# A two-layer decoder trunk in split fp32 on one core: one-function Gelu, an earlier spatial turn, earlier sums, and one more Strassen unit in the last pair

## The chip, the cores and the metric

The kernel runs on one core of a Trainium2 chip. The time is the device time of that core in microseconds (us), the median over several executions. TensorE (PE) does the matrix products, VectorE (DVE) and ScalarE (ACT) prepare their operands and take up their results, GpSimd (POOL) and SyncE (SP) mainly issue DMAs. "L245" is line 245 of the kernel before; an executed instruction carries the line that recorded it.

## The reference

Tokens x (256 x 2048, fp32) go through two layers:

```python
def chunked_sgu(uv, w_s, b_s, ln_g, ln_b):
    ...
    u, v = uv[..., :SGU_WIDTH], uv[..., SGU_WIDTH:]
    ... # vn: v normalised in each group of 128 channels, times ln_g, plus ln_b
    w = jnp.where(tri[None], w_s, jnp.zeros_like(w_s))
    s = jnp.einsum('gij,bnjgd->bnigd', w, vc) + jnp.transpose(b_s)[None, None, :, :, None]
    return u * s.reshape(B, S, SGU_WIDTH)

for l in range(DEPTH):
    h = rms_norm(x, mix_norm[l])
    q, k, v, uv, gate_logits = jnp.split(h @ w_in[l], cuts, axis=-1)
    ... # q and k: norm and rotation
    branch_a = sliding_window_attention(q, k, v, sinks[l]) @ w_attn_branch[l]
    branch_b = chunked_sgu(jax.nn.gelu(uv), w_spatial[l], b_spatial[l],
                           sgu_ln_g[l], sgu_ln_b[l]) @ w_sgu_branch[l]
    gates = jax.nn.sigmoid(gate_logits)
    merged = gates[..., :D_MODEL] * branch_a + gates[..., D_MODEL:] * branch_b
    x = x + merged @ w_out[l]
    h2 = rms_norm(x, ffn_norm[l])
    x = x + (jax.nn.silu(h2 @ w_gate[l]) * (h2 @ w_up[l])) @ w_down[l]
```

`jax.nn.gelu` is here the form with a tanh: 0.5 x (1 + tanh(0.798 (x + 0.0447 x^3))).

## The kernel before, in words

**Products.** All large products run in fp32 accuracy by a high and a low part of each operand. A weight half of 256 rows by 512 columns is one *entry*: its DMA (L218, 512 KB, on SP) fills `raw`, ScalarE rounds it to `whi` (L244), VectorE subtracts to get `wlo` (L245), and TensorE multiplies the stationary activation parts `uh` and `ul` with them (add_product, L340 and L341): six matmuls of 128x512 for one tile of 128 tokens (hi*hi, hi*lo and lo*hi for two blocks of 128 rows), so 12 for both tiles. The pool of `whi` and `wlo` has four buffers (W_SPLIT = 4): the split of an entry starts when TensorE has finished the entry four places earlier.

**Strassen units.** A *unit* is 512 rows of weights against a pair of column chunks, done by seven products of six matmuls (P1 to P7, 42) in place of eight (48). Its weight sums are made by VectorE (L229), its activation sums by `transposed` (L421 to L509): `flat` (L480), `whole` (uh on ScalarE and ul on VectorE, L484 and L485), four `sums` on VectorE (L499), and `finished` (sh on ScalarE, sl on VectorE, L484 and L485). After P5 ScalarE copies the accumulators (L363 to `kept`, L364 to the other accumulator), after P6 and P7 VectorE adds to `kept` (L366). A block that is in no unit has only `uh` and `ul`, made in two halves (ScalarE L435, VectorE L436). `pair` builds the entries of two column chunks; with `two=True` it takes two units.

**Time slots.** `tick()` closes a slot of 12 matmuls, `after(n, fn)` records `fn` n slots later. `wino=` gives six such delays, for the two halves of `flat`, `whole`, the two pairs of `sums`, and `finished`. TensorE's instructions run in the order in which they are recorded; on the other engines a scheduler sets the order when the program is built, and each engine then keeps to it.

**A layer.** First the input projection, with attention and the gating unit worked in between. Class `Spatial` has the gating unit: for the two chunks of v and of u it copies half of the scaled projection from PSUM (L811) and forms Gelu with a Square (L818) and a Tanh (L821) on ScalarE and two operations on VectorE (L819, L822), for each of the two token tiles apart. v is normalised (`center`, `scaled`, `shifted`, L835 to L856), and `mix` multiplies with the transposed spatial weights. These come from `spatial` (L648 to L654): eight transposes by TensorE into `pw` and two VectorE copies to `wsT`. Attention turns its probabilities on TensorE as well (`ppt`, L783); `pw` and `ppt` share two PSUM buffers. Then the branch products, the output projection, and the feed-forward part in three rounds of 4, 4 and 3 chunks of 512 (ROUNDS): `hidden` makes each chunk of the hidden activations (silu L981, product L985/L986), turns it, and after each round `residual` multiplies with `w_down` in two pairs of column chunks and adds to the residual `xs` (L888). In the last round there are three blocks, of which the first (WINO = 0) is a Strassen unit.

Of the kernel before, what the change touches and what calls it, by code (L numbers as in the profile page):

```python
# [10 lines left out]
AF = mybir.ActivationFunctionType  # L11
# [4 lines left out]
NT = 2  # L16
# [21 lines left out]
WINO_MIX = 6, 7, 9, 10, 11, 13  # L38
WINO_HID = 7, 8, 17, 18, 19, 20
W_SPLIT = 4  # L40
W_TWO = 24
# [11 lines left out]
              for early in ([(("q", 1),), (("gate", 0),)], [(("q", 1), ("gate", 0))])]  # L53
GELU_A = 0.044715
GELU_C = 0.7978845608028654


@with_exitstack
def hybrid_trunk(ctx: ExitStack, tc: tile.TileContext, x, mix_norm, w_in, q_norm, k_norm, sinks,
# [101 lines left out]
    for l in range(DEPTH):  # L161
# [14 lines left out]
        for r, (f0, f1) in enumerate(ROUNDS):  # L176
            for f in range(f0, f1):
                plans.append(pair(("ffn", l), w_gate[l, :, f * CW:(f + 1) * CW], w_up[l, :, f * CW:(f + 1) * CW], f == 0,
                                  two=r > 0 and f - f0 < 3))
            c_ = cols_of(w_down[l, f0 * CW:f1 * CW, :], NCH)  # L180
            plans += [pair(("hid", l, r), c_[j], c_[j + 1], j == 0) for j in range(0, NCH, 2)]
    entries = []
# [79 lines left out]
    def after(n, fn):  # L262
        steps.append((slot_no[0] + n, fn))
# [399 lines left out]
    def fetch_large(pl):  # L663
        for n, i in ((13, 2), (17, 3), (21, 0), (25, 1)):
            after(n, lambda i=i: pl.fetch(i))
        after(40, pl.spatial)

# [132 lines left out]
    class Spatial:  # L800
# [5 lines left out]

        def half(self, ps, name):

            dst = slot([P, NT, CW], name=name)
            for t in range(NT):  # L810
                nc.scalar.activation(dst[:, t, :], ps[t], AF.Copy, scale=self.nrm.rh[t])  # L811
            return dst

        def gelu(self, dst, t):

            xh = dst[:, t, :]
            sq = temp(name="sq")
            nc.scalar.activation(sq, xh, AF.Square, scale=2.0)  # L818
            nc.vector.scalar_tensor_tensor(out=sq, in0=sq, scalar=1.0 / GELU_A, in1=xh,  # L819
                                           op0=ALU.add, op1=ALU.mult)  # L820
            nc.scalar.activation(sq, sq, AF.Tanh, scale=2.0 * GELU_C * GELU_A)  # L821
            nc.vector.scalar_tensor_tensor(out=xh, in0=sq, scalar=1.0, in1=xh, op0=ALU.add, op1=ALU.mult)  # L822

        def v(self, c, ps):
            self.vt[c] = vt = self.half(ps, "v")
            for t in range(NT):
                after(1 + t, lambda t=t: self.gelu(vt, t))
                after(4 + 3 * t, lambda t=t: self.center(c, t))
# [29 lines left out]
        def u(self, c, ps):  # L858
            ut = self.half(ps, "u")
            for t in range(NT):  # L860
                after(1 + t, lambda t=t: self.gelu(ut, t))
            for b in range(2):
                after(12 + 3 * b, lambda b=b: self.mix(c, b, ut))
            after(18 + 6 * c, lambda: transposed(self.sguT, c, ut, queue=nc.sync))
# [45 lines left out]
    for l in range(DEPTH):  # L910
# [65 lines left out]
        def hidden(hT, c):  # L976
# [6 lines left out]
            def on_up(up):  # L983
                for t in range(NT):
                    nc.vector.scalar_tensor_tensor(out=hid[:, t, :], in0=up[t], scalar=norm.r[t], in1=hid[:, t, :],  # L985
                                                   op0=ALU.mult, op1=ALU.mult)  # L986
                pe, soon = c == len(hT) - 1 == 2, c == 3
                after(3 if pe else 1 if soon else 2,
                      lambda: transposed(hT, c, hid, on_pe=pe, wino=WINO_HID if c == WINO else None,
                                         queue=None if soon else nc.gpsimd, late=-2 if soon else 0))  # L990
# [52 lines left out]
```

## Time and profile before

| | |
|---|---|
| Time, median of 3 executions | 2457.51 us (2455.78 to 2459.42) |
| The profiled execution's own time | 2457.45 us |
| Its span, first to last instruction | 2455.7 us |
| TensorE busy | 2438.1 us, 99% |
| VectorE busy | 1999.5 us, 81% |
| ScalarE busy | 1472.5 us, 60% |
| DMA | 506.74 MB, 206 GB/s on average |

Rows of the profile name the line, the engine, the operation, output and inputs (buffer numbers left out), the count and the mean of one; what stands in brackets or behind the last bar is the idle time of that engine before the instruction and what it waited for. A matmul's own duration (about 0.39 us) overlaps the next; the distance of their starts is what one costs. The columns of the windows view are busy time and count for each engine, then the granted clock of TensorE, the DMA share and GB/s.

### The profile page before, as it was taken

The numbers are of one execution on the slowest core, as the hardware profiler recorded it, in microseconds if no ns is written. First come the engines' busy times: TensorE is split into PE (matmuls) and PEld (weight loads), VectorE is DVE, ScalarE is ACT, GpSimd is POOL, SyncE is SP. The second block draws the span as 40 slices with busy tenths as digits, with TensorE's granted clock in tenths as the row PEclk, the third lists the DMA queues.
The fourth block names the chain that finished last, engine by engine and source line by source line (L and its number), as shares of the span: only waits on it lengthen the run. The fifth ranks groups of instructions, "written<-read, shape, count | busy, mean of one in ns | idle before, by whom it ended". The sixth has DMA issues, their size and how long they took to land.

```text
span 2455.7 us, 31363 instructions
## 1 busy us (share of the span) xinstructions
PE 2438.1 (99%) x10968; PEld 2012.6 (82%) x10968; DVE 1999.5 (81%) x2320; ACT 1472.5 (60%) x1842; POOL 315.6 (13%) x592
## 2 busy tenths in 40 slices
PE   9999999999999999999999999999999999999999
PEld 7888888888888888887887888888888888888877
DVE  6798676797978997899877986768878789978996
ACT  5567544576655665566655665545666556655664
POOL 3100002132210111001101000021322101110110
PEclk9999999999999999999999999999999999999999
DMA  9555657576667657665747446675767675667654
GB/s 299 196 187 163 212 198 220 186 236 210 220 217 233 210 176 231 230 203 170 229 155 257 152 157 223 202 215 177 246 202 236 204 245 189 200 209 241 203 179 139
DMA packets 280782, 506.74 MB, mean 206 GB/s; under 512 B 28272, under 2 KB 40144, under 8 KB 280624
## 3 DMA queue, kind: packets, MB, share of 16 engines
q1 hardware_dynamic: 262544, 486.35, 61.0%
q0 software_dynamic: 17760, 18.12, 2.8%
q8 instruction: 86, 1.41, 0.2%
q14 instruction: 72, 0.59, 0.1%
q10 hardware_dynamic: 320, 0.27, 0.0%
HBM read 475.27 MB, written 2.10 MB: 194 GB/s over the span
## 4 chain that ended last, share of the span: by engine, by line
PE 90%; DVE 3%; DMA 3%; SPq 1%; issue 1%; ACT 1%; DVEq 0%; ACTq 0%
PE acc L340 59%; PE acc L341 29%; DMA raw<-in_w_in_dram 2%; DVE wlo L245 2%; SPq L416 1%; ACT whi L244 1%; PE po L793 1%; PE psc L754 0%; PE ppt L783 0%; DVE raw L229 0%; PE psg L871 0%; PE pt L453 0%; DMA raw<-in_w_up_dram 0%; DMA raw<-in_w_down_dram 0%; DVE box L410 0%
## 5 line engine op out<-in xcount | busy, mean ns | idle before, releaser
L244 ACT ACTIVATE whi<-raw 128x1024 fp32r<-128x1024 f32 (+1 forms) x1074 | 1132.0, 1059 | 883.0 <-PE acc L341 623.4
L245 DVE TENSOR_TENSOR wlo<-raw,whi 128x1024 fp32r<-128x1024 f32 (+1 forms) x1075 | 1301.3, 1219 | 399.0 <-ACT whi L244 386.7
L340 PE MATMUL acc<-whi,uh 128*128 128x512 f32 x2994 | 1170.3, 391 | 1.2 <-ACT uh L439 1.2
L340 PE MATMUL acc<-wlo,uh 128*128 128x512 f32 x2994 | 1167.1, 390 | 3.0 <-DVE wlo L245 2.9
L341 PE MATMUL acc<-whi,ul 128*128 128x512 f32 x2994 | 1166.4, 390 | 0.0
L340 PEld LDWEIGHTS acc<-wlo,uh 128*128 128x128 f32 x2994 | 562.6, 188 | 123.2 <-DVE wlo L245 6.0
L340 PEld LDWEIGHTS acc<-whi,uh 128*128 128x128 f32 x2994 | 562.6, 188 | 117.7 <-ACT uh L439 1.4
L341 PEld LDWEIGHTS acc<-whi,ul 128*128 128x128 f32 x2994 | 562.3, 188 | 117.8 <-DVE ul L444 0.5
L416 POOL DMA_DIRECT2D tt<-box x544 | 266.5, 497 | 1697.0 <-ACT whi L244 695.5
L229 DVE TENSOR_TENSOR raw<-raw,raw 128x1024 f32<-128x1024 f32 x236 | 287.8, 1219 | 1.6 <-DMA raw<-in_w_up_dram 0.8
L341 PE MATMUL acc<-whi,sl 128*128 128x512 f32 x472 | 184.0, 390 | 3.2 <-DVE sl L485 3.2
L340 PE MATMUL acc<-whi,sh 128*128 128x512 f32 x472 | 184.8, 392 | 1.7 <-ACT acc L364 1.7
L340 PE MATMUL acc<-wlo,sh 128*128 128x512 f32 x472 | 184.2, 390 | 0.0
L341 PEld LDWEIGHTS acc<-whi,sl 128*128 128x128 f32 x472 | 88.6, 188 | 22.5 <-DVE sl L485 4.0
L340 PEld LDWEIGHTS acc<-whi,sh 128*128 128x128 f32 x472 | 88.6, 188 | 20.9 <-ACT acc L364 2.1
L340 PEld LDWEIGHTS acc<-wlo,sh 128*128 128x128 f32 x472 | 88.7, 188 | 18.0
L366 DVE TENSOR_TENSOR kept<-acc,kept 128x512 f32<-128x512 f32 x94 | 64.3, 684 | 10.1 <-PE acc L341 10.1
L369 ACT ACTIVATE acc<-kept 128x512 f32<-128x512 f32 x94 | 54.9, 586 | 4.3 <-DVE kept L366 4.2
L888 DVE SCALAR_TENSOR_TENSOR xs<-acc,xs 128x512 f32<-128x512 f32 (+1 forms) x66 | 42.0, 668 | 8.4 <-PE acc L341 8.1
L436 DVE TENSOR_TENSOR ul<-tt,uh 128x512 fp32r<-128x512 f32 x52 | 34.0, 684 | 2.9 <-ACT uh L435 2.9
L435 ACT ACTIVATE uh<-tt 128x512 fp32r<-128x512 f32 x52 | 29.8, 618 | 9.4 <-DMA tt<-box 9.4
L312 POOL TENSOR_TENSOR rv<-ve,neg_half 128x4 f32<-128x4 f32 x8 | 11.9, 1486 | 172.9 <-DVE ve L839 159.5
(137 smaller groups left out, 874.8 us busy)
## 6 DMA issues: line engine op xcount, KB each, us to landing
raw<-in_w_in_dram SPq DMA_DIRECT2D x239, 512.0 KB, 4.7
raw<-in_w_gate_dram SPq DMA_DIRECT2D x176, 512.0 KB, 4.4
raw<-in_w_up_dram SPq DMA_DIRECT2D x176, 512.0 KB, 4.9
raw<-in_w_down_dram SPq DMA_DIRECT2D x176, 512.0 KB, 5.0
raw<-in_w_out_dram SPq DMA_DIRECT2D x64, 512.0 KB, 5.0
tt<-box POOLq DMA_DIRECT2D x544, 32.0 KB, 4.2
raw<-in_w_attn_branch_dram SPq DMA_DIRECT2D x32, 512.0 KB, 5.6
raw<-in_w_sgu_branch_dram SPq DMA_DIRECT2D x32, 512.0 KB, 4.4
```

The lines of the kernel that those rows point to most:

```text
L229: self.last = nc.vector.tensor_tensor(out=self.raws[d], in0=self.raws[x], in1=self.raws[y], op=ALU.subtract)
L244: self.high = nc.scalar.activation(hi[:, i, :], raw[:, i, :], AF.Copy)
L245: self.last = nc.vector.tensor_tensor(out=lo[:, i, :], in0=raw[:, i, :], in1=hi[:, i, :].bitcast(F32), op=ALU.subtract)
L340: nc.tensor.matmul(ps, a, part[:, kk, :], start=first and kk + n == 0, stop=False, skip_group_check=True)
L341: nc.tensor.matmul(ps, b, hi[:, kk, :], start=False, stop=kk == 1, skip_group_check=True)
L366: nc.vector.tensor_tensor(out=p.kept[:, int(tag == "P7"), :], in0=a[1], in1=p.kept[:, 1, :], op=ALU.add)
L369: nc.scalar.activation(ps, p.kept[:, t, :], AF.Copy)
L416: q.dma_start(dst[j * B:(j + 1) * B, i], box[i * B:(i + 1) * B, j])
L435: nc.scalar.activation(h, s_, AF.Copy)
L436: nc.vector.tensor_tensor(out=l, in0=s_, in1=h.bitcast(F32), op=ALU.subtract)
L793: nc.tensor.matmul(po[:, h, :], pT[kb][:, h, :], self.kv[:, kb, KVW + g * HD:KVW + (g + 1) * HD], start=kb == 0, stop=kb == t)
L888: nc.vector.scalar_tensor_tensor(out=xs[:, t, sl], in0=sums[t][:, i * w:(i + 1) * w], scalar=scale, in1=xs[:, t, sl], op0=ALU.mult, op1=AL ...
```

## The change

1. `Spatial.half` and the old `gelu` go. The new `gelu` is one activation for each token tile, straight from PSUM with the norm as scale, tile 1 first.
2. `fetch_large` records `pl.spatial` 34 slots on in place of 40.
3. The one unit of a last round (three blocks) gets WINO_END in place of WINO_HID, in both layers.
4. The second pair of column chunks of the last round of the last layer has two units; its second unit is block 1, which takes WINO_END too and so gets `flat`, `whole`, `sums` and `finished` in place of the two halves.

```diff
 WINO_HID = 7, 8, 17, 18, 19, 20
+WINO_END = 7, 8, 12, 13, 14, 15
...
-            plans += [pair(("hid", l, r), c_[j], c_[j + 1], j == 0) for j in range(0, NCH, 2)]
+            plans += [pair(("hid", l, r), c_[j], c_[j + 1], j == 0, two=j > 0 and f1 == NF and l == DEPTH - 1)
+                      for j in range(0, NCH, 2)]
...
-        after(40, pl.spatial)
+        after(34, pl.spatial)
...
-        def half(self, ps, name):
+        def gelu(self, ps, name):
             dst = slot([P, NT, CW], name=name)
+            last = nc.scalar.activation(dst[:, 1, :], ps[1], AF.Gelu_apprx_tanh, scale=self.nrm.r[1])
+            with tc.issue_after(last.ins):
+                nc.scalar.activation(dst[:, 0, :], ps[0], AF.Gelu_apprx_tanh, scale=self.nrm.r[0])
+            return dst
+
+        def v(self, c, ps):
+            self.vt[c] = self.gelu(ps, "v")
             for t in range(NT):
-                nc.scalar.activation(dst[:, t, :], ps[t], AF.Copy, scale=self.nrm.rh[t])
-            return dst
-
-        def gelu(self, dst, t):
-            xh = dst[:, t, :]
-            sq = temp(name="sq")
-            nc.scalar.activation(sq, xh, AF.Square, scale=2.0)
-            nc.vector.scalar_tensor_tensor(out=sq, in0=sq, scalar=1.0 / GELU_A, in1=xh,
-                                           op0=ALU.add, op1=ALU.mult)
-            nc.scalar.activation(sq, sq, AF.Tanh, scale=2.0 * GELU_C * GELU_A)
-            nc.vector.scalar_tensor_tensor(out=xh, in0=sq, scalar=1.0, in1=xh, op0=ALU.add, op1=ALU.mult)
-
-        def v(self, c, ps):
-            self.vt[c] = vt = self.half(ps, "v")
-            for t in range(NT):
-                after(1 + t, lambda t=t: self.gelu(vt, t))
                 after(4 + 3 * t, lambda t=t: self.center(c, t))
...
-            ut = self.half(ps, "u")
-            for t in range(NT):
-                after(1 + t, lambda t=t: self.gelu(ut, t))
+            ut = self.gelu(ps, "u")
...
+                wino = None
+                if c == WINO:
+                    wino = WINO_HID if len(hT) == 4 else WINO_END
+                elif c == WINO + 1 and len(hT) == 3 and l == DEPTH - 1:
+                    wino = WINO_END
                 after(3 if pe else 1 if soon else 2,
-                      lambda: transposed(hT, c, hid, on_pe=pe, wino=WINO_HID if c == WINO else None,
+                      lambda: transposed(hT, c, hid, on_pe=pe, wino=wino,
                                          queue=None if soon else nc.gpsimd, late=-2 if soon else 0))
```

**ScalarE at the first v chunk of layer 2.** Numbers behind names are buffers, and each kernel numbers its own; `whi` are weight splits, `v` the chunk, `pT` and `pr` attention's probabilities, `sq` the scratch of the old Gelu. Before:

```order
L811 ACTIVATE v_11565<-acc_11382,rhalf_2070_10713 128x512
L811 ACTIVATE v_11565<-acc_11383,rhalf_2073_10720 128x512
L244 ACTIVATE whi_11619<-raw_11510 128x1024
L785 ACTIVATE pT_11610<-ppt_11605 128x512
L818 ACTIVATE sq_11612<-v_11565 128x512
L818 ACTIVATE sq_11638<-v_11565 128x512
L244 ACTIVATE whi_11649<-raw_11531 128x1024
L821 ACTIVATE sq_11612<-sq_11612 128x512
L821 ACTIVATE sq_11638<-sq_11638 128x512
L244 ACTIVATE whi_11665<-raw_11510 128x1024
L771 ACTIVATE pr_11581,den_11597<-pr_11581,negm_11592 128x128 x4
L768 ACTIVATE es_11594<-es_11594 128x4
```

After, with an ACT_TABLE_LOAD ahead of the Gelu and another ahead of the next exponentials (L771):

```order
L244 ACTIVATE whi_11522<-raw_11464 128x1024
L810 ACT_TABLE_LOAD
L810 ACTIVATE v_11538<-acc_11343,rstd_2064_10678 128x512
L812 ACTIVATE v_11538<-acc_11342,rstd_2061_10671 128x512
L244 ACTIVATE whi_11574<-raw_11483 128x1024
L785 ACTIVATE pT_11570<-ppt_11565 128x512
L771 ACT_TABLE_LOAD
L771 ACTIVATE pr_11541,den_11557<-pr_11541,negm_11552 128x128 x4
L768 ACTIVATE es_11554<-es_11554 128x4
L244 ACTIVATE whi_11599<-raw_11504 128x1024
L244 ACTIVATE whi_11615<-raw_11483 128x1024
```

Square and Tanh are gone, and the exponentials of the next attention step (L771) now stand ahead of the two next splits rather than behind them. In the whole program ScalarE has 18 table loads in place of 4: one ahead of each of the eight groups of Gelu, and one ahead of the next other function; SP's and GpSimd's lists keep their order except for the last output rows.

**VectorE at the spatial weights of layer 2.** `wsT` is the copy of the turned weights, `q` and `box` belong to the turn of the queries, `psc` are scores. Before:

```order
L245 TENSOR_TENSOR wlo_11494<-raw_11413,whi_11493 128x1024
L245 TENSOR_TENSOR wlo_11515<-raw_11431,whi_11514 128x1024
L245 TENSOR_TENSOR wlo_11534<-raw_11473,whi_11533 128x1024
L245 TENSOR_TENSOR wlo_11550<-raw_11491,whi_11549 128x1024
L654 COPY wsT_11568<-pw_11569 128x512
L654 COPY wsT_11568<-pw_11575 128x512
L758 TENSOR_TENSOR pr_11581<-psc_11582,mask 128x2x128
L245 TENSOR_TENSOR wlo_11620<-raw_11510,whi_11619 128x1024
L758 TENSOR_TENSOR pr_11581<-psc_11586,mask 128x2x128
```

After:

```order
L245 TENSOR_TENSOR wlo_11315<-raw_11254,whi_11314 128x1024
L410 STREAM_TRANSPOSE box_11334<-q_11186 128x4x4x32
L245 TENSOR_TENSOR wlo_11339<-raw_11273,whi_11338 128x1024
L410 STREAM_TRANSPOSE box_11334<-q_11186 128x4x4x32
L245 TENSOR_TENSOR wlo_11376<-raw_11293,whi_11375 128x1024
L654 COPY wsT_11391<-pw_11392 128x512
L654 COPY wsT_11391<-pw_11398 128x512
L245 TENSOR_TENSOR wlo_11407<-raw_11312,whi_11406 128x1024
L758 TENSOR_TENSOR pr_11422<-psc_11423,mask 128x2x128
L758 TENSOR_TENSOR pr_11422<-psc_11427,mask 128x2x128
```

The two copies have moved from behind the scores' step that TensorE's next `ppt` follows to a place some six slots earlier, between two splits; on TensorE the eight transposes into `pw` moved with them, from directly ahead of psc and ppt to between the entries of whi_11295 and whi_11314. In layer 1 TensorE's eight transposes moved in the same way, by six entries.

**VectorE at the end.** The last round of layer 2: `sums`, `sl` and `ul` are the activation sums and low parts of a unit, `hid` the product of L985 (now L973). Before, where the unit's `sl` stood (it serves the entry of whi_20206, its P5):

```order
L499 TENSOR_TENSOR sums_20185<-sums_20185,flat_19932 128x256
L245 TENSOR_TENSOR wlo_20207<-raw_20095,whi_20206 128x1024
L245 TENSOR_TENSOR wlo_20217<-raw_20166,whi_20216 128x1024
L499 TENSOR_TENSOR sums_20185<-flat_19932,sums_20185 128x256
L245 TENSOR_TENSOR wlo_20236<-raw_20188,whi_20235 128x1024
L229 TENSOR_TENSOR raw_20095<-raw_20192,raw_20095 128x1024
L485 TENSOR_TENSOR sl_20230<-sums_20185,sh_20229 128x1024
L245 TENSOR_TENSOR wlo_20256<-raw_20095,whi_20255 128x1024
L245 TENSOR_TENSOR wlo_20271<-raw_20190,whi_20270 128x1024
```

After, the `sl` of block 0 (sl_20018) stands ahead of wlo_20121 and wlo_20131, the splits of the entry before P5 and of P5 itself. Further on the work of the new unit has come in (block 1: ul_20022, sums_20346 and sl_20411):

```order
L366 TENSOR_TENSOR kept_20183<-acc_20146,kept_20183 128x512
L245 TENSOR_TENSOR wlo_20277<-raw_20226,whi_20276 128x1024
L973 TENSOR_SCALAR hid_20006<-acc_20091,rstd_2962_15234,hid_20006 128x512
L245 TENSOR_TENSOR wlo_20288<-raw_20240,whi_20287 128x1024
L973 TENSOR_SCALAR hid_20006<-acc_20092,rstd_2965_15241,hid_20006 128x512
L485 TENSOR_TENSOR ul_20022<-flat_20205,uh_20021 128x1024
L245 TENSOR_TENSOR wlo_20312<-raw_20254,whi_20311 128x1024
...
L499 TENSOR_TENSOR sums_20346<-flat_20205,sums_20346 128x256
L245 TENSOR_TENSOR wlo_20395<-raw_20254,whi_20394 128x1024
L245 TENSOR_TENSOR wlo_20415<-raw_20349,whi_20414 128x1024
L229 TENSOR_TENSOR raw_20240<-raw_20309,raw_20240 128x1024
L485 TENSOR_TENSOR sl_20411<-sums_20346,sh_20410 128x1024
```

Between the two pieces stand five splits, two weight sums (L229), three `sums` and two halves of block 2's `ul` (L436). TensorE's entries at that place, by the number of their `whi` and with their matmuls, are after the change: 20228 (6), 20244 (12, the end of block 2's up product, whose result hid_20006 takes), 20258 (6), 20276 (12, the first that uses ul_20022), 20287 (6), eight transposes of hid_20006, 20311 (6), 20325 (12), 20351 (6), 20384 (6), 20394 (6, P5 of the new unit, the first that uses sl_20411), 20414 (12). On ScalarE the copy L363 after the first P5 (entry 20130) stands directly behind whi_20173; before, the copies after that P5 (entry 20206) stood behind whi_20289, which waits for entry 20216, and L364 behind whi_20307 as well.

More of the change, by code (lines that the diff above doesn't have):

```diff
@@ L53 @@
               for early in ([(("q", 1),), (("gate", 0),)], [(("q", 1), ("gate", 0))])]
-GELU_A = 0.044715
-GELU_C = 0.7978845608028654
 @with_exitstack
```

## The prediction

> **What bounds the kernel now.** The page first, for the bound, then the waits of TensorE, then single stretches in the timeline.
>
> ```profile
> span 2455.7 us, 31363 instructions
> PE 2438.1 (99%) x10968; PEld 2012.6 (82%) x10968; DVE 1999.5 (81%) x2320; ACT 1472.5 (60%) x1842; POOL 315.6 (13%) x592
> ```
>
> TensorE sets the time. Work taken from VectorE or ScalarE alone brings nothing; only what removes a matmul or a wait of TensorE counts. Its waits, in all:
>
> ```profile
> PE acc L341 <- DVE sl L485: 3.2, 2, 1.6
> PE acc L340 <- DVE wlo L245: 2.9, 5, 0.8
> PE ppt L783 <- DVE wsT L654: 2.4, 1, 2.4
> PE acc L340 <- ACT acc L364: 1.7, 1, 1.7
> ```
>
> The columns are the sum, the times and the longest. Each of the four groups is touched by the change, and together they are 10.2 us: that is the room. The price of a matmul is the distance of starts, not the 0.39 us of its own row. In the piece below, 12 matmuls lie between the starts at 1337.74 and 1340.46: 2.72 us, or 0.227 each.
>
> ```profile
> 1337.74 0.39 PE L340 MATMUL acc<-wlo,uh 128*128 128x512 f32 x1
> ...
> 1340.46 0.39 PE L340 MATMUL acc<-wlo,uh 128*128 128x512 f32 x1
> ...
> 1340.91 1.03 PE L653 MATMUL pw<-ident,wsraw 128*128 128x128 f32 x8
> 1341.88 0.72 PE L754 MATMUL psc<-kT,qT 64*128 64x128 f32 x8
> 1345.03 0.66 PE L783 MATMUL ppt<-ident,pr 128*128 128x128 f32 x4 [2.43 <-DVE wsT L654]
> ...
> 1346.93 0.63 PE L340 MATMUL acc<-wlo,uh 128*128 128x512 f32 x1
> 1347.36 0.63 PE L341 MATMUL acc<-whi,ul 128*128 128x512 f32 x1
> ```
>
> **Part 2, the spatial turn (layer 2).** ppt needs a PSUM buffer that pw holds until VectorE has copied it, and VectorE copies only behind two splits. With the copies six slots earlier this wait of 2.43 us has no cause left: ppt's buffers were then free some 12 us before. What could be late next is pr, made from a score step five slots back, so nothing. Behind the wait matmuls start 0.43 apart instead of 0.227, and the granted clock (last but two columns) says why:
>
> ```profile
> 1345.00:1350.00 5.00, 4.97 (x17) 4.02 (x18) 5.00 (x8) 1.84 (x4) 0.00 (x0) 0.66 0.64 233
> ```
>
> In these 5 us the clock was 0.66, which loses 5 x 0.34 = 1.7 us. No other wait of TensorE is as long, and I take the dip to go with it: **-2.4 and -1.7 us**. [...]
>
> The eight transposes cost the same wherever they stand, except where TensorE then waits anyway. In both layers they now stand ahead of a stall on a split:
>
> ```profile
> 121.99 0.39 PE L340 MATMUL acc<-whi,uh 128*128 128x512 f32 x1
> 122.95 0.50 PE L340 MATMUL acc<-wlo,uh 128*128 128x512 f32 x1 [0.57 <-DVE wlo L245]
> 1322.58 0.47 PE L340 MATMUL acc<-whi,uh 128*128 128x512 f32 x1
> 1323.80 0.51 PE L340 MATMUL acc<-wlo,uh 128*128 128x512 f32 x1 [0.76 <-DVE wlo L245]
> ```
>
> That split waits for a load which SP issues late, behind 16 gathers for the queries' turn:
>
> ```profile
> 105.64 11.02 SPq L416 DMA_DIRECT2D tt<-box  x16
> 116.76 2.58 SPq L218 DMA_DIRECT2D raw<-in_w_in_dram  x5
> ```
>
> The load does not depend on pw, so pw's time fills the stall. By the starts the stalls are 122.95 - 121.99 - 0.23 = 0.73 us and 1323.80 - 1322.58 - 0.23 = 0.99 us; pw takes 0.97 us from its start to that of psc (above), hardly more than the second, so I count **-0.7 and -0.85 us**. If the load moved with TensorE, this gain would be nothing.
>
> **Part 1, Gelu.**
>
> ```profile
> L811 ACT ACTIVATE v<-acc,rhalf 128x512 f32<-128x512 f32 x8 | 5.3, 676 | 0.5 <-PE acc L341 0.5
> L818 ACT ACTIVATE sq<-u 128x512 f32<-128x512 f32 x8 | 5.0, 630 | 0.1
> L821 ACT ACTIVATE sq<-sq 128x512 f32<-128x512 f32 x16 | 9.8, 619 | 1.5 <-DVE sq L819 1.5
> L819 DVE SCALAR_TENSOR_TENSOR sq<-sq,v 128x512 f32<-128x512 f32 x8 | 5.4, 683 | 0.1
> L822 DVE SCALAR_TENSOR_TENSOR v<-sq,v 128x512 f32<-128x512 f32 x8 | 5.4, 680 | 0.0
> ```
>
> VectorE loses 16 x 0.683 + 16 x 0.680 = 21.8 us. ScalarE loses 16 x (0.676 + 0.63 + 0.619) = 30.8 us. It gains 16 Gelu, which the trace does not show: at least the 0.619 of Tanh, at most two passes, 1.36; I take 0.68, the row nearest in form (from PSUM with a scale by partition, L811), so 10.9 us, and have 9.9 and 21.8 as the ends. And it gains 14 table loads, which these rows price:
>
> ```profile
> 575.77 1.28 ACT L981 ACT_TABLE_LOAD   x1 [0.34 <-PE acc L341]
> 577.07 1.27 ACT L981 ACTIVATE hid<-acc,rstd 128x512 f32<-128x512 f32 x2
> ```
>
> The next activation starts 0.02 us behind the load, so 14 x 1.28 = 17.9 us. ScalarE's sum is then 2 us less: no more work, but lumpier, since a group is now a load, two Gelu and a load in 3.9 us. Whether that costs anything is decided by the split queued behind a group. In this stage ScalarE is ahead of TensorE:
>
> ```profile
> 1366.34 1.06 ACT L244 ACTIVATE whi<-raw 128x1024 fp32r<-128x1024 f32 x1 [1.86 <-PE acc L341]
> ```
>
> It waits for TensorE to free a buffer, four entries ahead of their use, mostly 10.9 us (4 x 2.72), and a split takes some 2.5 us on both engines. The loads fall into such waits, and the exponentials placed ahead of two splits end before those splits' buffers are free. VectorE, the tighter of the two here (47.4 us of 50 in the row below), has 2.7 us less to do for each chunk. TensorE does not wait here for anything that the old Gelu made. So **0 us**, from -0.5 (a short wait for att before the scores, which VectorE could now answer sooner) to +3.
>
> ```profile
> 1350.00:1400.00 50.00, 50.00 (x257) 41.02 (x256) 47.40 (x101) 35.49 (x70) 4.78 (x3) 1.00 0.50 159
> 2300.00:2350.00 50.00, 50.00 (x222) 41.44 (x221) 47.33 (x46) 32.75 (x38) 7.83 (x16) 1.00 0.58 185
> ```
>
> [...]
>
> **Part 3, the sums of a last round.**
>
> ```profile
> 2375.06 0.40 PE L340 MATMUL acc<-wlo,sh 128*128 128x512 f32 x1
> 2375.76 1.22 DVE L485 TENSOR_TENSOR sl<-sums,sh 128x1024 fp32r<-128x1024 f32 x1
> 2377.03 0.50 PE L341 MATMUL acc<-whi,sl 128*128 128x512 f32 x1 [1.58 <-DVE sl L485]
> ```
>
> P5's third matmul waits for sl; the starts lie 1.97 us apart (the one before at 2375.06), 1.75 over the beat. The waits view counts two such, one in each layer. With sl several splits ahead both go: **-1.75 twice**. The moved work is ul, four sums and sl. By the starts below one of VectorE's instructions overlaps the next by some 0.08 us, so a pass of 128x1024 (1.22) costs 1.14, a sum 0.34 and a hid 0.67; the moved work, 3.6 us, now lies where VectorE has little idle (47.33 of 50 above) and delays four splits by 1.1 to 1.8 us. Comparing the end of a wlo with the start of its first matmul gives slacks of 1.5 to 2.4 us in layer 2 and 1.2 to 2.2 in layer 1, so it costs about **+0.25** in layer 1, **+0.05** in layer 2.
>
> ```profile
> 2356.26 0.74 DVE L985 SCALAR_TENSOR_TENSOR hid<-acc,rstd,hid 128x512 f32<-128x512 f32 x1
> 2356.93 1.22 DVE L245 TENSOR_TENSOR wlo<-raw,whi 128x1024 fp32r<-128x1024 f32 x1
> ...
> 2368.74 0.42 DVE L499 TENSOR_TENSOR sums<-flat 128x256 f32<-128x256 f32 x1
> 2369.08 1.22 DVE L245 TENSOR_TENSOR wlo<-raw,whi 128x1024 fp32r<-128x1024 f32 x1
> ```
>
> **Part 4, the second unit.** It saves six matmuls: 6 x 0.227 = **-1.36 us**. The copies after P5 waited so far:
>
> ```profile
> 2381.04 1.06 ACT L244 ACTIVATE whi<-raw 128x1024 fp32r<-128x1024 f32 x1 [1.67 <-PE acc L341]
> ...
> 2383.05 0.57 ACT L363 ACTIVATE kept<-acc 128x512 f32<-128x512 f32 x1
> ...
> 2384.73 0.58 ACT L364 ACTIVATE acc<-acc 128x512 f32<-128x512 f32 x1
> ```
>
> In ScalarE's list they stood behind a split that waits for TensorE; the new list has L363 three entries earlier: **-1.84** (the wait of 1.7 and the slower start behind it).
>
> New are two waits. Entry 20276 needs ul_20022 in its third matmul, 8 matmuls (1.8 us) after the end of 20244. VectorE's list has ahead of ul kept, wlo_20277, hid, a split and hid: kept needs the end of 20228, 2.7 us before that of 20244, and is done at -1.8 us; then wlo_20277 takes 1.14, hid 0.67, the split 1.14, hid 0.67, ul 1.22. That ends at 3.0, late by 1.2, with the handovers 1.4 to 2.0. Entry 20394 needs sl_20411, 56 matmuls and the transposes (12.7 + 0.9 = 13.6 us) after 20244. From ul to sl VectorE has six splits, three weight sums, four sums, two halves of ul and sl, with no idle: 9 x 1.14 + 4 x 0.34 + 2 x 0.6 + 1.22 = 14.0, so 17.0 to 17.6: late by **3.4 to 4.0 us in all, +3.7**. Everything behind has slack again.
>
> So the second unit by itself gives back more than its six matmuls.
>
> **Sum.** -2.4 - 1.7 - 0.7 - 0.85 - 1.75 - 1.75 + 0.25 + 0.05 - 1.36 - 1.84 + 3.7 = -8.35 us. From the profiled execution's 2457.45 us, practically the median, that gives **2449.1 us**.
>
> **The rivals.** (a) *ScalarE becomes the bound in the attention stage.* If splits behind the Gelu groups have no room, each of the 14 loads lands on TensorE: at most 17.9 us, 2467.0. It is slower by the 0.2% of 4.9 us, about what a measurement here can tell from no change, once 11 of 14 loads do so (14.1 against 8.35 + 4.9 = 13.25). For it: the loads come in pairs around a Gelu, and VectorE is full there. Against: ScalarE is busy 35.5 us of 50 and waits for TensorE. (b) *The last pair is worse than I count*: the new unit's P5 copies wait again behind a split, as before (+1.84), and its sl once more behind one split and one weight sum (+2.3): 2453.2. For it: 18 splits and 8 weight sums, 29.6 us, stand against 132 matmuls, 29.9 us, so VectorE cannot catch up. (c) *The stalls stay*: loads move with TensorE and the clock still dips, +1.55 + 1.7 = 2452.3. (d) *The change does not bring the new waits*, since ul and sl run sooner than the list suggests: 2445.4.
>
> **Chances.** Forecast 0.55, (a) 0.08, (b) 0.15, (c) 0.12, (d) 0.10. The forecast's own terms span about 2446 to 2452.5 (Gelu +3, tail 0.3 either way, stalls). (d) at 2445.4 and (b) with a part of (a) widen this to 2444 to 2457. Faster by over 0.2% (below 2452.6): forecast without its edge 0.52, (d) 0.10, half of (c) 0.06, so 0.68. Within: (b) 0.15, the rest of (c) 0.06, an edge of the forecast 0.02, so 0.23. Slower: (a) and an unforeseen hundredth, 0.09.
>
> **What would show it.** Right: no wait of ppt for wsT and clock 1.00 throughout layer 2's attention; no wait for sl in a last round's first pair; in the last pair one wait for ul L485 of 1.2 to 2 us and one for sl L485 of about 2; 18 table loads with ScalarE's busy time about 2 us less and VectorE's about 22 us less there. Wrong: new waits for wlo between the v and u chunks (a), for acc L364 at the end (b), or a clock below 1 near 1345 (c).

## The result and the profile after

| | median | ratio to before, 95% interval |
|---|---|---|
| before | 2459.47 us (14 executions, 2455.78 to 2462.14) | |
| after | 2464.76 us (14 executions, 2461.15 to 2465.99) | 1.002 (1.0013 to 1.0028) |

The change makes the kernel 5.3 us slower; 2449.1 was forecast. The profiled execution took 2465.63 us, 8.2 more than that of before. The page of after:

```profile
span 2463.9 us, 31324 instructions
PE 2442.5 (99%) x10962; PEld 2013.9 (82%) x10962; DVE 1991.4 (81%) x2299; ACT 1475.5 (60%) x1831; POOL 316.3 (13%) x592
```

Six matmuls fewer, as planned, and TensorE is still busy 4.4 us longer: a first sign of a lower clock (the mean granted clock was 0.997, in before 0.999). TensorE's waits in after (sum, times, longest):

```profile
PE acc L340 <- ACT acc L364: 3.3, 1, 3.3
PE acc L340 <- DVE wlo L245: 3.1, 5, 1.0
PE acc L341 <- DVE ul L485: 2.7, 1, 2.7
PE acc L340 <- DVE kept L366: 2.3, 3, 1.6
PE acc L340 <- ACT uh L439: 2.0, 1, 2.0
PE acc L341 <- DVE sl L485: 1.9, 1, 1.9
```

The wait of ppt for wsT is gone and both old waits for sl are gone. In their place stand one for ul and one for a new sl, which were forecast, and one of 3.3 us for the copy L364 and three for `kept`, which were not. The granted clock (last but two columns) around the old wait of ppt, and behind three of the new waits:

```profile
1345.00:1350.00 5.00, 5.00 (x30) 3.95 (x29) 1.23 (x1) 3.20 (x4) 0.00 (x0) 1.00 0.99 351
1168.00:1173.00 5.00, 5.00 (x17) 3.91 (x16) 2.86 (x4) 1.87 (x2) 0.00 (x0) 0.66 0.63 204
2400.00:2405.00 5.00, 4.15 (x11) 3.35 (x12) 4.54 (x5) 0.64 (x2) 0.00 (x0) 0.66 0.94 324
2416.00:2421.00 5.00, 4.57 (x14) 3.60 (x15) 4.91 (x5) 2.56 (x4) 0.00 (x0) 0.69 0.55 189
```

One dip went, three came. Where the time went is read best by starts: a large matmul is the same one in both traces up to the last pair, so the difference of its two starts is the lag of after at that place. The change of the lag over each stage, beside the forecast's terms for it:

| stage (time in before) | forecast, us | measured, us |
|---|---|---|
| start, to 36 | 0 | +1.0 |
| layer 1, attention, to 316 | -0.7 | +3.6 |
| layer 1, last round, 1111 to 1230 | -1.75 + 0.25 | +3.0 |
| layer 2, spatial turn, to 1369 | -0.85 - 2.4 - 1.7 | -5.2 |
| layer 2, attention, to 1562 | 0 | +2.4 |
| layer 2, last round, first pair, 2333 to 2381 | -1.75 + 0.05 | -1.6 |
| layer 2, last pair, to the end | -1.36 - 1.84 + 3.7 | +5.1 |
| all | -8.35 | +8.2 |

Two stages came out as forecast (the turn and the first pair), four did not; the stretches left out changed by less than 0.1. The +1.0 of the start lies in this execution (the other runs have -0.2 to +2.2 there). Four places show the rest.

**Layer 1, last round.** ScalarE of after, with the idle time in brackets, then TensorE at the same place:

```profile
1161.57 1.06 ACT L244 ACTIVATE whi<-raw 128x1024 fp32r<-128x1024 f32 x1 [1.54 <-issue]
1164.29 1.06 ACT L244 ACTIVATE whi<-raw 128x1024 fp32r<-128x1024 f32 x1 [1.66 <-PE acc L341]
1165.25 1.13 ACT L435 ACTIVATE uh<-tt 128x512 fp32r<-128x512 f32 x2
1166.29 0.58 ACT L363 ACTIVATE kept<-acc 128x512 f32<-128x512 f32 x1
1166.90 0.58 ACT L364 ACTIVATE acc<-acc 128x512 f32<-128x512 f32 x1
```

```profile
1163.82 0.39 PE L341 MATMUL acc<-whi,ul 128*128 128x512 f32 x1
1167.53 0.50 PE L340 MATMUL acc<-whi,sh 128*128 128x512 f32 x1 [3.33 <-ACT acc L364]
```

The copies L363 and L364 stand in ScalarE's list behind two splits that wait for TensorE to finish entries *after* P5, and behind uh. (The row of the first split names no releaser, but it starts 0.08 us after the end of the first entry behind P5, whose last matmul ran from 1161.10 to 1161.49, and the second starts as long after the end of the next entry.) ScalarE of before at this place:

```profile
1158.48 0.58 ACT L363 ACTIVATE kept<-acc 128x512 f32<-128x512 f32 x1
1159.20 1.06 ACT L244 ACTIVATE whi<-raw 128x1024 fp32r<-128x1024 f32 x1
1160.17 0.58 ACT L364 ACTIVATE acc<-acc 128x512 f32<-128x512 f32 x1
```

There no such split stood ahead of L363, and only one, with hardly a wait, ahead of L364, which ended 0.9 us before TensorE needed it. In after TensorE's starts are 3.71 us apart, 3.5 over the beat, and the clock then dips (0.66 from 1168 to 1173, above): together they take back the 1.75 of sl and some 3.0 more.

**Attention.** The groups of table loads and Gelu on ScalarE came out at the prices that were assumed (sum, mean ns):

```profile
L810 ACT ACT_TABLE_LOAD x8 | 10.3, 1283 | 0.1
L771 ACT ACT_TABLE_LOAD x6 | 7.7, 1283 | 0.1
L810 ACT ACTIVATE v<-acc,rstd 128x512 f32<-128x512 f32 x4 | 2.8, 689 | 0.7 <-PE acc L341 0.6
```

What had not been looked at is who else waits for ScalarE. VectorE's waits for attention's exponentials, in before:

```profile
DVE den L773 <- ACT pr L771: 3.7, 3, 1.6
DVE den L773 <- ACT es L768: 1.0, 2, 0.7
```

and in after:

```profile
DVE den L773 <- ACT pr L771: 10.4, 6, 2.8
DVE den L773 <- ACT es L768: 6.0, 3, 4.3
```

4.7 us have become 16.4. ScalarE at the longest of them, and VectorE's den:

```profile
128.77 1.28 ACT L810 ACT_TABLE_LOAD   x1
130.06 0.69 ACT L810 ACTIVATE v<-acc,rstd 128x512 f32<-128x512 f32 x1
130.65 0.68 ACT L812 ACTIVATE v<-acc,rstd 128x512 f32<-128x512 f32 x1
131.35 1.28 ACT L768 ACT_TABLE_LOAD   x1
132.65 0.20 ACT L768 ACTIVATE es<-es 128x4 f32<-128x4 f32 x1
```

```profile
132.88 0.16 DVE L773 TENSOR_TENSOR den<-den,es 128x4 f32<-128x4 f32 x1 [4.28 <-ACT es L768]
...
158.16 0.68 DVE L366 TENSOR_TENSOR kept<-acc,kept 128x512 f32<-128x512 f32 x1
```

A small exponential of 0.20 us stands behind load, Gelu, Gelu, load: 3.9 us, and VectorE stands still for 4.28. It has not caught up by 158: TensorE waits there for `kept` (1.60 us in its row).

**The last pair.** VectorE of after, the split ahead of ul and its load on ScalarE, and TensorE:

```profile
2395.42 0.75 DVE L973 SCALAR_TENSOR_TENSOR hid<-acc,rstd,hid 128x512 f32<-128x512 f32 x1
2397.78 1.23 DVE L245 TENSOR_TENSOR wlo<-raw,whi 128x1024 fp32r<-128x1024 f32 x1 [1.61 <-ACT whi L244]
2398.92 0.74 DVE L973 SCALAR_TENSOR_TENSOR hid<-acc,rstd,hid 128x512 f32<-128x512 f32 x1
2399.58 1.21 DVE L485 TENSOR_TENSOR ul<-flat,uh 128x1024 fp32r<-128x1024 f32 x1
```

```profile
2396.69 2.00 ACT L244 ACTIVATE whi<-raw 128x1024 fp32r<-128x1024 f32 x2 [3.28 <-DMA raw<-in_w_down_dram]
```

```profile
2397.79 0.39 PE L340 MATMUL acc<-wlo,uh 128*128 128x512 f32 x1
2400.85 0.80 PE L341 MATMUL acc<-whi,ul 128*128 128x512 f32 x1 [2.68 <-DVE ul L485]
...
2414.09 0.39 PE L340 MATMUL acc<-wlo,sh 128*128 128x512 f32 x1
2416.43 0.50 PE L341 MATMUL acc<-whi,sl 128*128 128x512 f32 x1 [1.95 <-DVE sl L485]
```

By the starts the waits cost 3.06 - 0.23 = 2.8 and 2.34 - 0.23 = 2.1 us. With 1.36 and 1.84 saved, the stage's +5.1 needs 8.3 us of new cost; the 3.4 beyond the two waits is what the two dips take (a dip is some 8 matmuls at 0.43 in place of 0.227, 1.6 us).

### The profile page after: what moved, and what is told of

Same layout as the page of the kernel before. It is cut to its first block, busy times and chain, and to the rows that moved or that the text cites. A ratio compares the mean times of both kernels' runs of the same rounds, so it can differ in the third digit from the quotient of the medians.

```text
span 2463.9 us, 31324 instructions
## 1 busy us (share of the span) xinstructions
PE 2442.5 (99%) x10962; PEld 2013.9 (82%) x10962; DVE 1991.4 (81%) x2299; ACT 1475.5 (60%) x1831; POOL 316.3 (13%) x592
## 4 chain that ended last, share of the span: by engine, by line
PE 89%; DVE 4%; DMA 2%; issue 2%; ACT 1%; SPq 1%; POOL 0%; DVEq 0%; ACTq 0%; POOLq 0%
PE acc L340 58%; PE acc L341 29%; DMA raw<-in_w_in_dram 2%; DVE wlo L245 2%; SPq L416 1%; ACT whi L244 1%; DVE raw L229 1%; PE po L793 1%; PE psc L754 0%; PE ppt L783 0%; PE pt L453 0%; DMA raw<-in_w_down_dram 0%; DVE kept L366 0%; POOL rv L312 0%; DVE pr L758 0%
## 5 line engine op out<-in xcount | busy, mean ns | idle before, releaser
L229 DVE TENSOR_TENSOR raw<-raw,raw 128x1024 f32<-128x1024 f32 x240 | 292.7, 1220 | 1.9 <-DMA raw<-in_w_up_dram 1.0
L771 ACT ACTIVATE pr<-pr,negm 128x128 f32<-128x128 f32 (+1 forms) x64 | 28.4, 444 | 16.2 <-DVE negm L764 16.0
L436 DVE TENSOR_TENSOR ul<-tt,uh 128x512 fp32r<-128x512 f32 x50 | 32.8, 686 | 5.2 <-ACT uh L435 5.1
```

Source lines behind the costliest of these rows:

```text
L229: self.last = nc.vector.tensor_tensor(out=self.raws[d], in0=self.raws[x], in1=self.raws[y], op=ALU.subtract)
L436: nc.vector.tensor_tensor(out=l, in0=s_, in1=h.bitcast(F32), op=ALU.subtract)
L771: nc.scalar.activation(pr4[:, h, :nk], pr4[:, h, :nk], AF.Exp, bias=nm_[:, h:h + 1], accum_out=den[:, h:h + 1])
```

## The experiments

Each ran beside before; given are the medians of this / before in us and the ratio with its 95% interval. The diffs show only the piece of a line that changes. Theories at the start: **T1**, the new Gelu costs TensorE time through ScalarE's loads; **T2**, the sums' new place moves ScalarE's copies behind waiting splits; **T3**, the second unit's waits are those of VectorE's list. The rival throughout was that a part costs nothing by itself and the time is lost elsewhere.

### The four parts alone

**e1_gelu**: part 1 alone, that is the lines of `Spatial` in the change's diff:

```diff
-        def half(self, ps, name):
+        def gelu(self, ps, name):
...
```

> Part 1 (Gelu) alone on the kernel before. Theory: the one-function Gelu rearranges VectorE's and ScalarE's lists in the attention stages, so that new waits for kept L366 and for wlo appear there (the profile after shows some 6 us of them between 150 and 300 us and 1370 and 1530 us); the kernel is then 3 to 7 us slower than before. Rival: these waits come from the earlier spatial turn and not from Gelu; then this kernel is within 1 us of before, with no wait for kept.

2459.83 / 2459.69, 1.0 (0.9991 to 1.0009). T1 as stated then fails: by itself Gelu costs nothing. The waits of TensorE are nearly as before, that of ppt included (2.8). VectorE's waits for the exponentials have grown here too, to 12.7 us for pr and 0.3 for es, so a longer wait of VectorE alone does not decide.

**e2_spatial**: part 2 alone.

```diff
-        after(40, pl.spatial)
+        after(34, pl.spatial)
```

> Part 2 (spatial turn 34 slots on) alone. Theory: ppt's wait for wsT (2.4 us), the clock dip behind it (1.6) and the two load stalls (0.7 and 0.9) go, and nothing comes: 4.5 to 6 us faster than before. Rival: the moved copies bring the waits for kept and wlo in the attention stages; then it is between 1 us faster and 3 us slower.

2454.88 / 2459.69, 0.9983 (0.9974 to 0.9991). The wait of ppt is gone, and by stages the profiled execution gains 5.1 in the turn, no less than the 4.95 that were forecast for wait, dip and stall together. But it gives back 2.2 in the attention behind it, layer 1's 0.7 does not come (+0.4), and 2.0 of the gain arise in the last pair, which part 2 does not touch. There the scheduler put the copies one split sooner; ScalarE of e2:

```profile
2377.15 1.06 ACT L244 ACTIVATE whi<-raw 128x1024 fp32r<-128x1024 f32 x1 [1.32 <-PE acc L341]
2378.11 1.14 ACT L435 ACTIVATE uh<-tt 128x512 fp32r<-128x512 f32 x2
2379.16 0.58 ACT L363 ACTIVATE kept<-acc 128x512 f32<-128x512 f32 x1
```

Before, one more split with a wait of 1.67 stood ahead of L363. So part 2 itself is worth about 2.8 us, not the 5.65 forecast, and that -4.8 lies so near to the forecast is in part luck.

**e3_sums**: part 3 alone.

```diff
-wino=WINO_HID if c == WINO else None
+wino=None if c != WINO else WINO_HID if len(hT) == 4 else WINO_END
```

> Part 3 (WINO_END for the unit of a last round) alone. Theory: both waits for sl go (1.75 us each) and in layer 2 that for the copy L364 (1.84), but in layer 1 the copies after P5 now stand behind splits and uh, a wait of 3.3 us with a clock dip of 1.5 us behind it: 0 to 1.5 us faster in all. Rival: the wait for L364 in layer 1 belongs to the whole change; then it is 5 us faster.

2462.95 / 2459.69, 1.0011 (1.0002 to 1.0019): slower, against both. Both waits for sl went; one wait for the copy came in *each* layer (L365 is the L364 of before):

```profile
PE acc L341 <- ACT acc L365: 6.7, 2, 3.3
```

**e4_unit**: part 4 alone.

```diff
-j == 0) for j in range(0, NCH, 2)]
+j == 0, two=j > 0 and f1 == NF and l == DEPTH - 1) for j in range(0, NCH, 2)]
...
-wino=WINO_HID if c == WINO else None
+wino=WINO_HID if c == WINO else WINO_END if c == 1 and len(hT) == 3 and l == DEPTH - 1 else None
```

> Part 4 (second unit in the last pair, its block with WINO_END) alone; the unit of block 0 keeps its late sums. Theory: six matmuls go (1.36 us), but ul and sl of the new unit are late by 2.8 and 2.1 us with a clock dip of 1.5 us behind each: 3 to 7 us slower than before. Rival: the tail is dear only because part 3 put more work ahead of it; then it is within 1.5 us of before.

2465.76 / 2459.69, 1.0023 (1.0014 to 1.0032). Its waits:

```profile
PE acc L343 <- DVE sl L487: 6.8, 3, 3.7
PE acc L343 <- DVE ul L487: 2.3, 1, 2.3
```

Two of the three for sl are the old ones, so the new unit brings 3.7 and 2.3. With -1.36 and -1.84 that is +2.8; the measured 6.1 needs 3.3 more, by an estimate two dips of the length in after; the mean granted clock of the profiled execution was 0.997, that of before 0.999. The four parts alone make +4.7 us in sum, the whole +5.3.

### Where ScalarE's copies stand

**e5_copies, e6_sums_copies, e8_after_copies**: a split that is the fifth or later entry behind P5 has to stand behind P5's copies; on before, on part 3 alone, and on the whole change.

```diff
-            nc.scalar.activation(a[0], a[1], AF.Copy)
+            stream.gate = (stream.at - 1 + W_SPLIT, nc.scalar.activation(a[0], a[1], AF.Copy))
...
-                        self.high = nc.scalar.activation(hi[:, i, :], raw[:, i, :], AF.Copy)
+                        with ExitStack() as st:
+                            if self.gate is not None and len(self.parts) > self.gate[0]:
+                                st.enter_context(tc.issue_after(self.gate[1].ins))
+                            self.high = nc.scalar.activation(hi[:, i, :], raw[:, i, :], AF.Copy)
```

> The kernel before, with one order added on ScalarE: from the fifth entry behind a P5 on, a split is issued behind that P5's copies (L363, L364). Theory (the copies' place in ScalarE's list makes the wait for acc L364): the 1.84 us in layer 2 go and nothing else changes, 1 to 2.5 us faster than before. Rival (the wait only moves to the wait for sl or to the splits behind): within 0.7 us of before.

2457.23 / 2459.36, 0.9994 (0.9985 to 1.0003).

> Part 3 alone with the same order added for the copies. Theory: the two waits of 3.5 us for acc L364 and the two clock dips behind them (1.6 and 2.0 us) go, and both waits for sl stay gone: 4 to 6 us faster than before, 8 to 10 faster than part 3 alone. Rival (VectorE is full there, so the earlier sums cost what they gain whatever ScalarE's list is): within 1.5 us of before, with waits for wlo or kept in their place.

2453.22 / 2459.36, 0.9974 (0.9964 to 0.9984).

> The whole change with the same order added for the copies. Theory: of the whole change's loss of 5.3 us the wait for acc L364 in layer 1 (3.5 us) and the clock dip behind it (1.5 us) go: within 1.5 us of before. Rival (another instruction comes late in its place): 4 us or more slower than before.

2459.99 / 2459.36, 0.9999 (0.9991 to 1.0008).

T2 is settled by e3 and e6. With the order alone (e5) 2.1 us went; the interval reaches no change, but the profiled execution gained its 2.0 in the last pair, where the wait of before was. With part 3 under it (e6) 6.1, which is 9.4 less than part 3 without it (e3: +3.3). ScalarE of e6 at the end, where e3 had two waiting splits ahead of the copies:

```profile
2381.64 0.58 ACT L368 ACTIVATE kept<-acc 128x512 f32<-128x512 f32 x1
2382.25 0.58 ACT L369 ACTIVATE acc<-acc 128x512 f32<-128x512 f32 x1
2382.75 2.95 ACT L249 ACTIVATE whi<-raw 128x1024 fp32r<-128x1024 f32 x3
```

On the whole change (e8) the order gives back 4.7. There the last pair cost 7.9, with a wait of 5.5 for ul: its load came later still.

### What the table loads cost

**e7_gelu_spatial**: parts 1 and 2, the edits of e1 and e2.

> Parts 1 and 2 together. Theory (the two add up, as 0.1 and -4.8 us): 3.5 to 6 us faster than before, with waits of 2 us in all for kept and wlo in the attention stages. Rival (the lists of the attention stages become bad only with both, as the 6 us of such waits after the whole change suggest): within 1.5 us of before, with 5 us or more of such waits.

2457.67 / 2459.36, 0.9992 (0.9983 to 1.0001). Part 2 alone made -4.8. Of the 3.1 between them 2.0 are the copies, which stand here as in before; the other 1.1 lies within the intervals, so the medians alone do not show that Gelu costs something beside part 2. The stages and the next run do.

**e9_no_loads**: e7 with Tanh in place of Gelu. The gating unit then computes other values; the lists of all engines stay, but the 14 table loads go.

```diff
-AF.Gelu_apprx_tanh
+AF.Tanh
```

> Parts 1 and 2 with Tanh in place of Gelu (the gating unit's values are then others): the same lists on every engine, but without the 14 table loads. Theory: the loads stand ahead of the exponentials on ScalarE, and VectorE, whose den waits for these, loses the time that Gelu freed (its waits for den rose from 3.7 us before to 16.3 us); without the loads these waits fall below 9 us, the waits of TensorE for kept and wlo in layer 1's attention stage mostly go, and the kernel is 2 to 4 us faster than parts 1 and 2, 4 to 6 faster than before. Rival (the order of the lists makes the waits, the loads are hidden): as parts 1 and 2, 1 to 2.5 us faster than before.

2454.09 / 2459.03, 0.9977 (0.9969 to 0.9986). VectorE's waits for the exponentials in e9:

```profile
DVE den L773 <- ACT pr L771: 8.7, 5, 2.1
DVE den L773 <- ACT es L768: 2.0, 2, 1.4
```

The loads cost 3.2 us of time (-1.7 against -4.9), and the stages say where: layer 1's attention +2.1 in e7, -1.0 in e9; layer 2's attention behind the turn +1.9 and -0.7. T1 holds, but only beside part 2. VectorE's waits for the exponentials are still 10.7 us without the loads, above the 4.7 of before, and cost nothing.

**e11_es**: e7 with the small exponential es ahead of the large ones and Gelu behind them.

```diff
-            nc.scalar.activation(es, es, AF.Exp)
+            es_ = nc.scalar.activation(es, es, AF.Exp)
...
+                with tc.issue_after(es_.ins):
+                    exps[0] = nc.scalar.activation(pr4[:, h, :nk], ...)
...
+            with tc.issue_after(exps[0].ins):
+                last = nc.scalar.activation(dst[:, 1, :], ps[1], ...)
```

> Parts 1 and 2, with es issued ahead of an attention step's exponentials and Gelu behind them; all table loads stay. Theory: the wait of den for es (5.9 us of VectorE, 4.3 at once at 132 us) goes, and with it 1 to 2 us of TensorE's waits for kept: 2.5 to 4 us faster than before. Rival (any load ahead of the next exponentials costs the same): as parts 1 and 2, 1 to 2.2 us faster than before.

2456.43 / 2459.03, 0.9992 (0.9984 to 1.0001). The waits for es went (5.9 to 0), those for pr hardly grew (10.4 to 11.4), and the median is within the error of e7, so as a cure this is not shown; the mean granted clock of the profiled execution was 0.998 besides, that of e7 0.999. But its stages show what the long wait for es did: layer 1's attention has +0.3 in place of e7's +2.1, and TensorE's waits for `kept` there are 0.3 us in place of 2.2. In layer 2's attention nothing is won (+2.4 against +1.9).

### The second unit's place, and the parts together

**e10_three**: parts 2 and 3 with the copies' order, old Gelu, no second unit: the edits of e2, e3 and e5.

> Parts 2 and 3 with the order for the copies, without Gelu and without the second unit. Theory (they lie in different stages and add up, -4.8 and -6.1): 9 to 12 us faster than before, the fastest so far. Rival (VectorE gives it back): less than 7 us faster.

2450.84 / 2459.03, 0.9967 (0.9954 to 0.9979). The 8.2 us lie between the two expectations. The sum of -4.8 and -6.1 counted the copies of the last pair twice; without e2's 2.0 for them it is -8.9.

**e12_tail**: e10 and the second unit (the `two=` of e4), with its ul, sums and sl recorded sooner.

```diff
+WINO_ONE = 7, 8, 9, 10, 11, 12
...
+wino=WINO_ONE if c == 1 and len(hT) == 3 and l == DEPTH - 1 else ...
```

> Parts 2 and 3 with the order for the copies, and the second unit in the last pair with its work earlier: whole, sums and finished at 9, 10, 11 and 12 in place of 12 to 15. Theory (the second unit is dear only because ul and sl stand too far back in VectorE's list): the waits for them fall below 1.5 us in all and the dips go, so that it is within 1.5 us of the kernel without the second unit. Rival (VectorE has no room in the last pair, or the unit's eight loads come late, as the wait of ScalarE for raw of 3.3 us at 2396 in the profile after suggests): 4 us or more slower than without it.

2450.16 / 2459.03, 0.9965 (0.9951 to 0.9978). No wait for ul or sl is left:

```profile
PE acc L347 <- DVE wlo L252: 4.0, 5, 1.5
PE acc L347 <- DVE kept L373: 1.3, 2, 0.9
```

The saved 1.36 us of matmuls show as 0.7 in the median, within the error. Of the kernels that compute the reference's values this has the lowest median: 8.9 us under before, where after is 5.3 over it.

**e13_after_tail, e14_mended, e15_mended_no_loads**: the whole change with that place of the unit (e13), with the copies' order as well (e14), and that with Tanh for Gelu, which again computes other values (e15). The edits are those of e12 (block 1's `WINO_END` becomes `WINO_ONE`), e5 and e9.

> The whole change, with the new unit's whole, sums and finished at 9, 10, 11 and 12 in place of 12 to 15. Theory (their place in VectorE's list makes the waits for ul and sl): of the 8 us that the last pair loses some 6.5 go, so 0 to 2.5 us faster than before. Rival (no room, or late loads): 3.5 us or more slower than before, with waits for wlo in place of those for ul.

2456.71 / 2459.37, 0.9989 (0.998 to 0.9998).

> The same with the order for the copies after P5 as well: all four parts, with two places mended. Theory (the causes add up: 5.3 - 6.5 - 4.7): 4 to 7.5 us faster than before. Rival: within 2 us of before.

2451.95 / 2459.37, 0.9971 (0.9961 to 0.9982).

> The same with Tanh in place of Gelu (other values in the gating unit), so without the 14 table loads. Theory (the loads cost some 3.6 us by VectorE's wait for the exponentials): 7.5 to 11 us faster than before, near the 8.35 of the forecast and beyond it. Rival: as with Gelu within 1.2 us.

2447.1 / 2459.37, 0.9952 (0.9938 to 0.9965).

T3 holds: the sooner place is worth 8.0 us on the whole change (+5.3 to -2.7), the copies' order 4.8 more, the loads 4.9 more (every execution of e15 is faster than every one of e14). VectorE of e14, where ul now stands directly behind `kept`, ahead of the split with the late load and of both hid:

```profile
2385.63 0.69 DVE L371 TENSOR_TENSOR kept<-acc,kept 128x512 f32<-128x512 f32 x1 [0.48 <-PE acc L346]
2386.24 1.22 DVE L490 TENSOR_TENSOR ul<-flat,uh 128x1024 fp32r<-128x1024 f32 x1
```

## Why the prediction was wrong, point by point

The change of the lag by stage, worked out as above for the profiled execution of each run (us):

| run | L1 attention | L1 last round | L2 turn | L2 attention | first pair | last pair |
|---|---|---|---|---|---|---|
| e1 (part 1) | +0.7 | -0.1 | -0.1 | -0.4 | +1.2 | 0.0 |
| e2 (part 2) | +0.4 | -0.1 | -5.1 | +2.2 | 0.0 | -2.0 |
| e7 (1, 2) | +2.1 | +1.6 | -5.2 | +1.9 | +0.7 | 0.0 |
| e9 (e7, no loads) | -1.0 | -0.1 | -5.2 | -0.7 | +3.4 | 0.0 |
| e11 (e7, es first) | +0.3 | +1.5 | -5.2 | +2.4 | +2.1 | 0.0 |
| e3 (part 3) | -0.3 | +4.2 | 0.0 | 0.0 | -1.1 | +3.3 |
| e6 (3, copies) | +0.3 | -2.1 | +1.5 | 0.0 | -2.0 | -1.2 |
| e12 (2, 3, 4 sooner, copies) | 0.0 | -1.8 | -5.2 | +2.4 | -2.0 | -1.5 |
| e13 (all, 4 sooner) | +2.9 | +3.2 | -5.2 | +1.2 | -1.2 | -1.2 |
| e14 (e13, copies) | +2.7 | -1.7 | -5.2 | +1.6 | -2.2 | -1.6 |
| e15 (e14, no loads) | 0.0 | -2.0 | -5.1 | -0.2 | -2.1 | -1.6 |

Single executions carry 1.5 us here and there, in stages whose waits of TensorE before has too: the +1.5 and +1.6 of e11 and e7 in layer 1's last round, parts of e9's +3.4 and e11's +2.1, and e6's +1.5. In e9's first pair the clock was 0.77 from 2375 to 2380, where before had 1.00; the wait for sl is as long in both (1.6).

**Right.** The spatial turn: -2.4, -1.7 and -0.85 were forecast, -5.1 to -5.2 came, in every run with part 2. Both waits for sl went in every run with part 3, and the copies' wait of layer 2 went. Gelu costs 0.69 a tile, and 14 table loads of 1.283 us came; the next activation starts 0.02 us after a load's end, as at 131.35 and 132.65 above.

**Wrong, 1: "-1.75 twice ... +0.25 in layer 1".** The slacks of the delayed splits were weighed, but moving the sums also moved ScalarE's copies L363 and L364, and the text checked their new place only in layer 2 ("the new list has L363 three entries earlier"). In layer 1 they fell behind two splits. e3 has the fault in both layers, e6 with the order has it in neither: +4.2 against -2.1. The price was in before already, 1.7 us for one such split. Worth 4.5 us.

**Wrong, 2: "So 0 us" for Gelu.** The step asked whether the split behind a group has room and whether TensorE waits for what Gelu makes. Neither fails. What fails is VectorE: it stops for the exponentials behind the loads, and more than half of the freed 21.8 us is lost again in waits (4.7 to 16.4 us). e9 and e15 take the loads alone away: in layer 1's attention 3.1 and 2.7 us, in layer 2's 2.7 and 1.8, and 3.2 and 4.9 in the medians. In layer 1 the one long wait for es is more than half of that: e11 takes it away and the stage falls by 1.8, while e1, with 12.7 us of waits for pr and only 0.3 for es, loses nothing clear. Which of the waits costs in layer 2 is not shown. Rival (a) had the right engine and its loads, but the wrong victim. Against the old Gelu (e12) the new one costs 2.7 in layer 1's attention (e14) and nothing in layer 2.

**Wrong, 3: "pw's time fills the stall".** It does, as the turn in layer 2 shows, but the gain does not last: runs with part 2 and the old Gelu (e2, e12) have 0.4 and 0.0 in layer 1 in place of -0.7, and +2.2 and +2.4 behind the turn of layer 2. VectorE is full there (47.4 us of 50 in the prediction's row), so time saved on TensorE is taken back when TensorE reaches VectorE's next result: in layer 2's attention e2 has waits of TensorE for `kept` (1.0) and wlo (0.9) which before has not. There only e9 and e15, which relieve VectorE *and* have no loads, keep the gain; in layer 1 e9 does (-1.0), but e15 has 0.0. That VectorE's fullness is the cause is argued from these rows; no run gave VectorE more room by itself.

**Wrong, 4: the size of "+3.7".** The mechanism was right, ul and sl late by VectorE's list, and e12 to e14 remove it by moving the unit in that list. The size was 4.9 by starts, and behind each wait came a dip (0.66 and 0.69, above) that was taken off for the old wait of ppt but added for none of the new ones: 3.4 more. VectorE's 1.61 us of waiting for the split ahead of ul, whose load landed late, was not in the sum either. In the rows above ul follows that split and one hid without a pause, so by an estimate 1.61 of ul's 2.68 us are the late load and 1.07 the list, near the 1.2 of the prediction. No run separates the two: the sooner place takes ul past both.

The sum fell at these four: 4.5 (copies), 6.6 (both attention stages) and 4.6 (last pair); with 0.9 from the start of the execution and the small differences that is the 16.6 between -8.35 and +8.2. The median itself differs by less, +5.3.

## What to carry to other kernels

When a change moves work, look up the new place of *every* instruction that waits, in each engine's list and at each repetition of the stage; an accident of the scheduler (one or two waiting splits ahead of a copy) was worth 2 to 5 us here, as much as each intended gain, and it also moved in runs that did not touch it (e2). For work put on an idle engine, ask which busy engine waits for the next thing in that queue. Price a new wait of TensorE with the clock dip that may follow it, 1.7 us each behind three waits of 1.95 to 3.33 us here.

## What the runs showed of the hardware

Behind some of its waits TensorE ran at half clock for a while. In the profiled executions of before and after these are, beyond the first 15 us, all distances of 1.9 us or more between matmul starts, with the idle time in them:

| start of the matmul behind, us | distance, us | idle, us | granted clock then |
|---|---|---|---|
| before, 1155.19 | 1.97 | 1.58 | 1.00 from 1156 to 1161 |
| before, 1345.03 | 2.70 | 2.43 | 0.50 from 1345.88 to 1349.29 |
| before, 2377.03 | 1.97 | 1.58 | 1.00 from 2377 to 2382 |
| before, 2385.36 | 2.07 | 1.68 | 1.00 from 2386 to 2391 |
| after, 158.89 | 1.99 | 1.60 | 1.00 from 159 to 164 |
| after, 1167.53 | 3.71 | 3.33 | 0.50 from 1168.59 to 1172.00 |
| after, 2400.85 | 3.06 | 2.68 | 0.50 from 2400.80 to 2404.21 |
| after, 2416.43 | 2.34 | 1.95 | 0.50 from 2417.87 to 2421.28 |

Each of the four dips is 3.41 us at 0.50, which loses 1.7 us. Behind the wait of 3.3 us for the copy in layer 1 the clock was 0.86 from 1163 to 1168 and 0.80 from 1168 to 1173 in e13, again 1.7 us, but 0.50 and 0.82 in e3, twice as much.

The length of the wait alone does not decide. In e4 a wait for ul of 2.33 us (a distance of 2.72) had no dip: up to 2403.43, 3.54 us on, matmuls start 0.23 apart but for the first. In e9 the wait for sl is 1.6 us long, as in before, and the clock was 0.77 from 2375 to 2380. What decides is not shown.
